# A swiglu's input product taken as seven products of quarters, in a two-block kernel of one core

## The chip, the core and the metric

The kernel runs on one core of one Trainium2 chip. Its time is the device time of one launch in microseconds (us), the median of several runs. TensorE is called PE, VectorE DVE, ScalarE ACT and GpSimd POOL, as in the profile; SP is the queue that starts the weight DMAs.

## The reference

Two transformer blocks follow each other. The first has two layers over 512 tokens and, in its first layer, 256 context tokens; each layer ends in a swiglu over a normed and modulated input. The second block (a short convolution, a dilated attention, a squared-relu MLP) isn't touched. What is changed here is the first product of this function, in both layers, with D = 1024 and FF = 2816:

```python
def swiglu(h, w_in, w_out):
    gt, up = jnp.split(h @ w_in, 2, axis=-1)
    return (jax.nn.silu(gt) * up) @ w_out
...
        hf = rms_norm(x, norm_ffn[l]) * (1.0 + sc_f) + sh_f
        x = x + g_f * swiglu(hf, ffn_w_in[l], ffn_w_out[l])
...
            hcf = rms_norm(ctx, norm_ffn[l]) * (1.0 + csc_f) + csh_f
            ctx = ctx + cg_f * swiglu(hcf, ffn_w_in[l], ffn_w_out[l])
```

## The kernel before, in words

Everything is float32. A product of two float32 matrices is made of three matmuls in a faster, rounded type (`fp32r`): each factor is split into a high part (a cast on ACT) and a low part (the rest, a subtraction on DVE), and high·high, high·low and low·high are added up in PSUM (`product`, L265, its matmuls on L273, L275 and L277).

**Weights.** `Weights` brings them in blocks of up to 2048 columns. `load` starts the DMA into one of two `wst` buffers, `split` casts it to `whi` on ACT (L91) and takes the low part `wlo` on DVE (L92), two buffers each, and `ahead` (L102) does both for the steps to come. The model is a list of steps (`Builder.step`, `Builder.run`); the instructions of the steps are then put in order on each engine by a scheduler, which looks at what depends on what, so that work of a later step can stand ahead of work of an earlier one.

**Tokens.** The activations lie transposed, as 8 tiles `x(k)` of 128 features by the tokens. Layer 0 has 768 of them (512 in `XT`, 256 in `XC`), layer 1 has 512.

**The input of the swiglu.** The last step of the mixer ahead of it calls `feed_mod(k, n)` for each tile k as soon as its residual is done. It adds the squares for the norm (ACT L327, then POOL L328) and makes the scaled tile's high part `nmh` (ACT L597) and low part `nml` (DVE L598). The scale by 1/rms comes after the product (`rstd`, `rbcast`, `nmr`), the shift as extra columns of the moving side.

**The swiglu (`swiglu`, L603).** Of the 2816 hidden features a tile has 128, so there are 22 tiles. For each one, a step `up` brings one weight block (8 k-tiles of the gate's columns and 8 of the up side's) and makes two products. In layer 0 that is 48 matmuls of 512 columns and 48 of 256 or 258; in layer 1 it is 96 of 256 or 258. DVE multiplies both results by `nmr` (L649), ACT takes the silu (L651), DVE adds the shift and multiplies (L652), and the result is split into `uh` and `ul`. The tiles come in parts of 8, 7 and 7; after each part four steps `down` multiply the part by the second weight matrix and add to the residual (L450). PE has enough to do in a `down` while the last tile's `uh` is finished, because the scheduler puts the next part's first `up` product ahead of it.

Of the kernel before, what the change touches and what calls it, by code (L numbers as in the profile page):

```python
# [45 lines left out]
def blk(w, k0, kt, c0, n):  # L46

    return w[k0 * P : (k0 + kt) * P, c0 : c0 + n].rearrange("(k p) n -> p k n", p=P), kt, n


def cols(views):

    ((h, l),) = views
    return [(h[:, :, c : c + P], l[:, :, c : c + P]) for c in range(0, h.shape[2], P)]


class Weights:
# [21 lines left out]
    def split(self, i):  # L79
        b = self.b  # L80
        nc = b.nc
        stage, n = self.loaded[i]
        self.loaded[i] = None
        desc, raw = self.desc[i]
        if raw:
            ((_, kt, m),) = desc
            self.done.append(stage[:, :n].rearrange("p (k n) -> p k n", k=kt))
            return
        hi = b.wpool.tile([P, 2048], FR, tag="whi", name="whi", bufs=WSP)
        lo = b.wpool.tile([P, 2048], FR, tag="wlo", name="wlo", bufs=WSP)  # L90
# [29 lines left out]
class Builder:  # L120
# [346 lines left out]
    def ada_first(self):  # L467
# [111 lines left out]
    def open_mod(self, l, side):  # L579


        n = L if l else T
        self.enter("nm", nm=(1, None, side))
        parts = [self.nm.tile([P, KT, n + 32], FR, name=m) for m in ("nmh", "nml")]
        self.feeds = parts + [self.nm.tile([P, n], F32, name="nmr"), self.nm.tile([P, KT, 4], F32, name="nmg")[:, :, 0:2]]
        self.gains(l, 1, self.feeds[3])
        self.split(self.M[:, l, 24:32, :], *(a[:, :, n : n + 2] for a in parts))

    def feed_mod(self, k, n):

        nc = self.nc
        hi, lo, _, G = self.feeds
        for z, (c0, m) in enumerate([(0, L)] + ([(L, C)] if n > L else [])):
            self.squares(k, c0, m, nc.gpsimd)
            g = G[:, k, z : z + 1]
            h = hi[:, k, c0 : c0 + m]
            nc.scalar.activation(h, self.x(k, c0, m), AF.Copy, scale=g)  # L597
            nc.vector.scalar_tensor_tensor(  # L598
                lo[:, k, c0 : c0 + m], self.x(k, c0, m), g, h.bitcast(F32), ALU.mult, ALU.subtract
            )  # L600


    def swiglu(self, l):  # L603
        wi, wo = self.I["ffn_w_in"][l], self.I["ffn_w_out"][l]
        n = T if l == 0 else L
        if l == 1:
            self.step(lambda: self.open_norm(("norm_mix_2", 0)))
        self.scope_step("ffn", hid=(1, None))

        if n == T:  # L610
            segs, at = [(0, L), (L, C + 2)], [(0, L), (L, T + 2)]
            tokens = lambda a: a[:, 0:T]
# [12 lines left out]
        parts = [(0, 8), (8, 7), (15, 7)]
        for q, (t0, nt) in enumerate(parts):

            def alloc():
                self.uh = self.hid.tile([P, 8, n], FR, tag="uh", name="uh")
                self.ul = self.hid.tile([P, 8, n], FR, tag="ul", name="ul")  # L630

            self.step(alloc)
            for i in range(nt):

                def up(v, i=i, start=q == 0 and i == 0):
                    nc = self.nc
                    rb = self.feeds[2]
                    og = product(v[0])
                    if start:
                        self.rstd(n)  # L640
                    ou = product(v[1])
                    if start:
                        nc.scalar.copy(rb, self.rbcast(n)[:, 0:n])
                    s, u = self.t(n), self.t(n)
                    sh = self.tmp.tile([P, 2, 2], F32, tag="sh", name="sh")
                    c = runs[0][1]
                    for y, o, d in ((0, og, s), (1, ou, u)):
                        nc.vector.tensor_copy(sh[:, y], o[:, c : c + 2])
                        nc.vector.tensor_tensor(tokens(d), tokens(o), tokens(rb), ALU.mult)  # L649
                    for z, (run, _) in enumerate(runs):  # L650
                        nc.scalar.activation(run(s), run(s), AF.Silu, bias=sh[:, 0, z : z + 1])  # L651
                        nc.vector.scalar_tensor_tensor(run(s), run(u), sh[:, 1, z : z + 1], run(s), ALU.add, ALU.mult)  # L652
                    self.split(s, self.uh[:, i, :], self.ul[:, i, :])

                self.step(up, (blk(wi, 0, KT, (t0 + i) * P, P), blk(wi, 0, KT, FF + (t0 + i) * P, P)))
            for i in range(0, KT, 2):

                def down(v, i=i, q=q, nt=nt):
                    if n == T:
                        outs = self.full(cols(v), self.uh, self.ul, 0, nt)  # L660
                    else:
                        o = self.pair(cols(v), self.uh, self.ul, 0, nt)
                        outs = [o[:, 0:L], o[:, L : 2 * L]]
                    for j in range(2):
                        k = i + j
                        self.residual(outs[j][:, 0:L], k, 0, L, self.mod(l, 5, k, 0))
                        if n == T:
                            self.residual(outs[j][:, L:T], k, L, C, self.mod(l, 5, k, 1))
                        if q == 2:
# [1670 lines left out]
```

## Time and profile before

| | |
|---|---|
| median of 3 runs | 3637.14 us (3633.1 to 3637.61) |
| profiled execution | 3626.45 us, its span 3624.4 us |
| PE busy | 3495.5 us (96%) |
| DVE busy | 1807.6 us (50%) |
| ACT busy | 1187.7 us (33%) |
| POOL busy | 72.0 us (2%) |
| chain of waits, by engine | PE 91%, DVE 4%, ACT 2%, DMA 1% |

The profile is one execution; its span runs from the first instruction to the last. An engine is busy while it executes an instruction. The rows called windows give the busy time of each engine in a stretch and the granted clock of PE there (1.00 is full speed). The chain of waits follows the end of the run back through what released each instruction.

### The profile page before, as it was taken

The page shows a single profiled execution, that of the slowest core. Times are in us where ns is not written, and L with a number is a line of the kernel's source. Part 1 is how long each engine was busy: PE and PEld are TensorE (multiplying, and loading weights), DVE is VectorE, ACT ScalarE, POOL GpSimd, SP SyncE. Part 2 cuts the span into 40 slices and gives each one's busy share as a digit, 9 for nine tenths or more (in the row PEclk, how much of TensorE's full clock was granted, in tenths as well). Part 3 has the DMA queues.
Part 4 walks back from the last instruction along what each step waited for, and adds up shares of the span by engine and source line. Part 5 has one row for each costly group of instructions (what it writes and reads, how often), then busy time and mean ns, then how long its engine had stood idle before and what let it go on. Part 6 is the DMA issues. An engine that isn't in the chain of part 4 may idle for free.

```text
span 3624.4 us, 46788 instructions
## 1 busy us (share of the span) xinstructions
PE 3495.5 (96%) x19754; PEld 3013.2 (83%) x19754; DVE 1807.6 (50%) x3145; ACT 1187.7 (33%) x1810; POOL 72.0 (2%) x87
## 2 busy tenths in 40 slices
PE   6999899999999989999999999999999999999998
PEld 4767777888888879988999888888889999988886
DVE  5657555653233345565444555444554444454445
ACT  4356545432121233343222322222334234222222
POOL 0000000020000001001000000000000000000000
PEclk9999999999999999999999999999999999999999
DMA  6111455422222223222333233333232222233332
GB/s 232 48 57 65 147 165 190 138 59 70 59 64 59 66 85 82 74 63 82 94 89 100 85 88 106 98 99 93 87 102 77 83 71 76 75 95 93 93 98 71
DMA packets 351873, 333.17 MB, mean 92 GB/s; under 512 B 22192, under 2 KB 293296, under 8 KB 351664
## 3 DMA queue, kind: packets, MB, share of 16 engines
q1 hardware_dynamic: 330320, 313.88, 27.8%
q10 hardware_dynamic: 21344, 16.30, 1.5%
q8 instruction: 155, 2.54, 0.3%
q14 instruction: 54, 0.44, 0.0%
HBM read 312.62 MB, written 15.96 MB: 91 GB/s over the span
## 4 chain that ended last, share of the span: by engine, by line
PE 91%; DVE 4%; ACT 2%; DMA 1%; issue 1%; SPq 0%; POOL 0%; ACTq 0%; DVEq 0%
PE ps L277 19%; PE ps L275 19%; PE ps L273 19%; PE ps L310 5%; PE ps L312 5%; PE ps L311 5%; PE ps L1332 3%; PE ps L1704 1%; PE ps L1705 1%; PE ps L1706 1%; PE psc L1332 1%; PE ds L986 1%; PE pp L273 1%; PE pp L275 1%; PE pa L515 1%
## 5 line engine op out<-in xcount | busy, mean ns | idle before, releaser
L91 ACT CAST whi<-wst 128x2048 fp32r<-128x2048 f32 (+5 forms) x245 | 442.1, 1805 | 1281.5 <-PE ps L275 910.9
L92 DVE TENSOR_TENSOR wlo<-wst,whi 128x2048 fp32r<-128x2048 f32 (+5 forms) x245 | 529.8, 2162 | 157.3 <-ACT whi L91 150.2
L275 PE MATMUL ps<-ul,whi 128*128 128x512 f32 (+1 forms) x1040 | 361.9, 375 | 0.0
L277 PE MATMUL ps<-uh,wlo 128*128 128x512 f32 (+1 forms) x1040 | 361.4, 375 | 0.0
L273 PE MATMUL ps<-uh,whi 128*128 128x512 f32 (+1 forms) x1040 | 359.8, 374 | 0.0
L277 PE MATMUL ps<-nhh,wlo 128*128 128x512 f32 x864 | 340.1, 394 | 0.0
L275 PE MATMUL ps<-nhl,whi 128*128 128x512 f32 x864 | 338.0, 392 | 0.0
L273 PE MATMUL ps<-nhh,whi 128*128 128x512 f32 x864 | 337.0, 390 | 0.0
L275 PE MATMUL ps<-nml,whi 128*128 128x258 f32 (+2 forms) x1408 | 322.7, 310 | 2.3 <-DVE nml L598 2.0
L273 PE MATMUL ps<-nmh,whi 128*128 128x258 f32 (+2 forms) x1408 | 319.9, 309 | 4.2 <-ACT nmh L597 4.2
L277 PE MATMUL ps<-nmh,wlo 128*128 128x258 f32 (+2 forms) x1408 | 322.5, 310 | 0.6 <-DVE wlo L92 0.6
L310 PE MATMUL ps<-whi,nhh 128*128 128x512 f32 x576 | 238.0, 413 | 0.0
L273 PEld LDWEIGHTS ps<-nmh,whi 128*128 128x128 f32 x1408 | 216.8, 188 | 20.8 <-issue 4.6
L275 PEld LDWEIGHTS ps<-nml,whi 128*128 128x128 f32 x1408 | 216.4, 189 | 18.4 <-DVE nml L598 4.1
L277 PEld LDWEIGHTS ps<-nmh,wlo 128*128 128x128 f32 x1408 | 216.7, 189 | 16.2 <-DVE wlo L92 0.9
L311 PE MATMUL ps<-wlo,nhh 128*128 128x512 f32 x576 | 230.2, 400 | 0.0
L312 PE MATMUL ps<-whi,nhl 128*128 128x512 f32 x576 | 229.9, 399 | 0.0
L275 PEld LDWEIGHTS ps<-ul,whi 128*128 128x128 f32 x1040 | 184.1, 188 | 38.3
L273 PEld LDWEIGHTS ps<-uh,whi 128*128 128x128 f32 x1040 | 183.0, 188 | 36.6
L277 PEld LDWEIGHTS ps<-uh,wlo 128*128 128x128 f32 x1040 | 183.6, 188 | 35.5
L275 PEld LDWEIGHTS ps<-nhl,whi 128*128 128x128 f32 x864 | 162.2, 188 | 37.5
L273 PEld LDWEIGHTS ps<-nhh,whi 128*128 128x128 f32 x864 | 162.2, 188 | 35.4
(439 smaller groups left out, 6037.1 us busy)
## 6 DMA issues: line engine op xcount, KB each, us to landing
wst<-in_ffn_w_in_dram SPq DMA_DIRECT2D x88, 512.0 KB, 4.9
wst<-in_ada_w_dram SPq DMA_DIRECT2D x42, 1024.0 KB, 5.2
wst<-in_attn_w_qkv_dram SPq DMA_DIRECT2D x36, 1024.0 KB, 5.1
wst<-in_mlp_w_up_dram SPq DMA_DIRECT2D x32, 1024.0 KB, 5.5
wst<-in_mlp_w_down_dram SPq DMA_DIRECT2D x32, 1024.0 KB, 5.0
wst<-in_even_w_in_dram SPq DMA_DIRECT2D x14, 1024.0 KB, 5.3
wst<-in_ffn_w_out_dram SPq DMA_DIRECT2D x16, 896.0 KB, 4.6
wst<-in_odd_w_in_dram SPq DMA_DIRECT2D x12, 1024.0 KB, 5.2
```

The lines of the kernel that those rows point to most:

```text
L91: nc.scalar.copy(hi[:, :n], stage[:, :n])
L92: nc.vector.tensor_tensor(lo[:, :n], stage[:, :n], hi.bitcast(F32)[:, :n], ALU.subtract)
L273: nc.tensor.matmul(outs[t][s], wh[:, k, :], xh[:, k0 + k, c0 : c0 + n], start=st, stop=False)
L275: nc.tensor.matmul(outs[t][s], wh[:, k, :], xl[:, k0 + k, c0 : c0 + n], start=False, stop=False)
L277: nc.tensor.matmul(outs[t][s], wl[:, k, :], xh[:, k0 + k, c0 : c0 + n], start=False, stop=sp)
L310: nc.tensor.matmul(o, lhs_h(4 * kk + k, 2 * i + j), wh[:, k, :], start=st, stop=False)
L311: nc.tensor.matmul(o, lhs_h(4 * kk + k, 2 * i + j), wl[:, k, :], start=False, stop=False)
L312: nc.tensor.matmul(o, lhs_l(4 * kk + k, 2 * i + j), wh[:, k, :], start=False, stop=sp)
L515: nc.tensor.matmul(ps[32 * k : 32 * k + 32, :], self.c2[:, a + 32 * k : a + 32 * k + 32], v[:, k, :], start=st, stop=sp,)
L986: nc.tensor.matmul(ps[:, o : o + w_], b.qkT[0][rows, h, j * P : (j + 1) * P], b.qkT[1][rows, h, c0 : c0 + w_], start=True, stop=True,)
L1332: mark = nc.tensor.matmul(out, lhsT, rhs, start=start, stop=stop)
L1704: nc.tensor.matmul(o, b.hh[:, k, at], wh[:, k, :], start=k == 0, stop=False)
```

## The change

Strassen's algorithm (in the form with seven products) replaces the plain product of a hidden tile. The weight block of a tile is seen as 2 by 2 quarters: a11 and a12 are the gate's columns of the first and the last four k-tiles, a21 and a22 the up side's. The input is seen as 2 by 2 quarters too: rows are the first or last four k-tiles, columns the first or the second half of the tokens (384 each in layer 0, 256 in layer 1), with two shift columns added. Seven products of quarters, each of 4 k-tiles and three matmuls, make 84 matmuls of 386 columns (layer 0) or 258 (layer 1).

- `combine` (new): for each tile POOL makes four sums of weight quarters, each 128x512, in `ws`, which has one buffer: s1 = a21+a22, s2 = s1−a11, s4 = a12−s2, s3 = a11−a21. Then seven factors of 512 columns are split (ACT L278, DVE L279) into both pairs of `whi` and `wlo`: a11, a12, s1 and s4 into the first, s2, s3 and a22 into the second.
- `quarters` (new, L323 ff.): the seven products in the order b11, t1, b21, b22, t2, t4, t3 of their input factor, into three PSUM regions R, Q and V, with copies from PSUM on ACT (L342, L344, L349, L353) and additions on DVE (L346, L350, L354, L355).
- `feed_mod`, through `scaled` and `factor`, now makes b11, t1, b21 and b22. A new step `mix_mod`, placed right ahead of the swiglu, makes t2, t4 and t3 in four rounds, from the scaled tiles of k and k+4, in four `t` tiles a round.
- The parts have 4 tiles in layer 0 (six parts, the last one of 2) and 6 in layer 1 (6, 6, 6 and 4). A `down` step has 4 tiles in layer 0 and 2 in layer 1. There are 96 residual additions in the swiglu of layer 0 (48 before) and 32 in that of layer 1 (24 before).

```diff
+        if raw == FAST:
+            self.done.append(self.combine(stage, desc))
+            return
...
+    def combine(self, stage, desc):
...
+        a11, a12, a21, a22 = (v[:, m, h] for m in range(2) for h in range(2))
+        ws = self.b.wpool.tile([P, 4, 4, P], F32, tag="ws", name="ws", bufs=1)[:, :, :q]
+        s1, s4, s2, s3 = (ws[:, i] for i in range(4))
+        nc.gpsimd.tensor_tensor(s1, a21, a22, ALU.add)
+        nc.gpsimd.tensor_tensor(s2, s1, a11, ALU.subtract)
+        nc.gpsimd.tensor_tensor(s4, a12, s2, ALU.subtract)
+        nc.gpsimd.tensor_tensor(s3, a11, a21, ALU.subtract)
+        out = {}
+        for names, srcs in ((("a11", "a12", "s1", "s4"), (v[:, 0], ws[:, 0:2])), (("s2", "s3", "a22"), (ws[:, 2:4], a22))):
...
+    def quarters(self, w, x, n, g, u):
...
+        one, two = self.ps(), self.ps()
+        R, Q, V = one[:, 0:n], one[:, L : L + n], two[:, 0:n]
...
+        add(R, "a11", "b11", True)
+        nc.scalar.copy(g[:, 0], R)
+        add(V, "s1", "t1", True)
+        nc.scalar.copy(u[:, 1], V)
+        add(Q, "a12", "b21", True)
+        nc.vector.tensor_tensor(g[:, 0], g[:, 0], Q, ALU.add)
+        add(V, "s4", "b22", False)
+        add(R, "s2", "t2", False)
+        nc.scalar.copy(g[:, 1], R)
+        nc.vector.tensor_tensor(g[:, 1], g[:, 1], V, ALU.add)
+        add(Q, "a22", "t4", True)
+        add(R, "s3", "t3", False)
+        nc.scalar.copy(u[:, 0], R)
+        nc.vector.tensor_tensor(u[:, 1], u[:, 1], R, ALU.add)
+        nc.vector.tensor_tensor(u[:, 0], u[:, 0], Q, ALU.add)
...
+        a, e = self.scaled(k, 0), self.scaled(k, 1)
+        if k < 4:
+            self.factor("b11", k, a)
+            nc.vector.tensor_tensor(e, e, a, ALU.subtract)
+            self.factor("t1", k, e)
+        else:
+            self.factor("b21", k, a)
+            self.factor("b22", k, e)
+
+    def mix_mod(self):
...
+        for k in range(4):
+            t = self.scaled(k, 0)
+            a, e = self.scaled(k + 4, 0), self.scaled(k + 4, 1)
+
+            b12 = self.scaled(k, 1)
+            nc.vector.tensor_tensor(t, b12, t, ALU.subtract)
+            nc.vector.tensor_tensor(t, e, t, ALU.subtract)
+            self.factor("t2", k, t)
+            nc.vector.tensor_tensor(t, a, t, ALU.subtract)
+            self.factor("t4", k, t)
+            nc.vector.tensor_tensor(t, e, b12, ALU.subtract)
+            self.factor("t3", k, t)
...
-        parts = [(0, 8), (8, 7), (15, 7)]
+        per = 4 if n == T else 6
+        parts = [(t0, min(per, FF // P - t0)) for t0 in range(0, FF // P, per)]
...
-            for i in range(0, KT, 2):
+            nb = 4 if n == T else 2
+            for i in range(0, KT, nb):
```

How it moves instructions, at three places. First, ACT at the start of layer 0's swiglu. L643 and the first L651 stand for the first hidden tile; before, nothing but a weight cast is between the last feed and them:

```order
L597 ACTIVATE nmh<-XC,nmg 128x256
L327 ACTIVATE t<-XT 128x512 [waits Pool_49]
L327 ACTIVATE t<-XC 128x256 [waits Pool_49]
L91 CAST whi<-wst 128x2048 [waits DMAHW5_49,DMAHW4_49,PE_49]
L643 COPY nmr<-ps 128x768 [waits PE_49]
L651 ACT_TABLE_LOAD
```

Now the same place; L342 and L344 are the copies out of PSUM of the first hidden tile, L676 and L677 make the scaled tiles of the last round of `mix_mod`, and L278 on `t2h`, `t4h`, `t3h` are its casts:

```order
L676 ACTIVATE t<-XT,nmg 128x128 [waits DVE_49]
L676 ACTIVATE t<-XC,nmg 128x256
L677 COPY t<-M 128x2
L278 CAST t2h<-t 128x386 [waits DVE_49]
L278 CAST t4h<-t 128x386 [waits DVE_49]
L342 COPY t<-ps 128x386 [waits Activation_49]
L278 CAST t3h<-t 128x386 [waits DVE_49]
L344 COPY t<-ps 128x386 [waits Activation_49]
L278 CAST whi<-wst 128x1024 [waits DMAHW2_49,PE_49]
L278 CAST whi<-ws 128x1024
L349 COPY t<-ps 128x386 [waits DVE_49,PE_49]
L751 ACT_TABLE_LOAD
```

The first tile's copy L342 now stands behind three of the four rounds of `mix_mod` and two thirds of the last one.

Second, DVE in one hidden tile of layer 1. Before:

```order
L648 COPY sh<-ps 128x2 [waits PE_49]
L649 TENSOR_TENSOR t<-ps,nmr 128x512
L648 COPY sh<-ps 128x2 [waits PE_49]
L649 TENSOR_TENSOR t<-ps,nmr 128x512
L652 SCALAR_TENSOR_TENSOR t<-t,sh 128x512 [waits DVE_49,Activation_49]
L92 TENSOR_TENSOR wlo<-wst,whi 128x2048 [waits DMAHW2_49,DMAHW1_49,Activation_49]
L243 TENSOR_TENSOR ul<-t,uh 128x512 [waits Activation_49]
```

Now, from the split of s2 and s3 of this tile to the split of a11 and a12 of the next one:

```order
L279 TENSOR_TENSOR wlo<-ws,whi 128x1024 [waits PE_49,Activation_49]
L279 TENSOR_TENSOR wlo<-wst,whi 128x512 [waits DMAHW4_49,Activation_49]
L354 TENSOR_TENSOR t<-t,ps 128x258 [waits Activation_49]
L355 TENSOR_TENSOR t<-t,ps 128x258
L747 TENSOR_TENSOR t<-t,nmr 128x2x256 [waits DVE_49]
L346 TENSOR_TENSOR t<-t,ps 128x258 [waits PE_49,Activation_49]
L752 SCALAR_TENSOR_TENSOR t<-t 128x256 [waits DVE_49]
L752 SCALAR_TENSOR_TENSOR t<-t 128x256
L279 TENSOR_TENSOR wlo<-wst,whi 128x1024 [waits DMAHW5_49,PE_49,Activation_49]
```

The weight split of the next tile, one instruction before, is now four, and its first one stands behind L747 and both L752, whose inputs all lie in SBUF.

Third, PE in a hidden tile of layer 0, at the end of the t2 product (`ps_7029` is this tile's PSUM with R and Q, `ps_7154` the next tile's; `whi_6750` holds s2, s3 and a22 of this tile, `whi_7015` a11 of the next):

```order
L336 MATMUL ps_7029<-t2l_6767,whi_6750 128x386
L336 MATMUL ps_7029<-t2h_6766,wlo_6751 128x386
L336 MATMUL ps_7154<-b11h_6412,whi_7015 128x386 [waits Activation_49]
L336 MATMUL ps_7154<-b11l_6413,whi_7015 128x386
L336 MATMUL ps_7154<-b11h_6412,wlo_7016 128x386 [waits DVE_49]
L336 MATMUL ps_7154<-b11h_6412,whi_7015 128x386
L336 MATMUL ps_7029<-t4h_6768,whi_6750 128x386 [waits Activation_49]
L336 MATMUL ps_7029<-t4l_6769,whi_6750 128x386
```

Four matmuls of the next tile's b11 product now stand ahead of this tile's last two products, t4 and t3, so these wait for the next tile's a11 and its low part.

## Rows read from the trace of the kernel before

**Rows 1.** The page: busy time, share of the span and instructions of three engines.

```profile
PE 3495.5 (96%) x19754; PEld 3013.2 (83%) x19754; DVE 1807.6 (50%) x3145; ACT 1187.7 (33%) x1810; POOL 72.0 (2%) x87
```

**Rows 2.** The page: the chain that ended last, share of the span by engine.

```profile
PE 91%; DVE 4%; ACT 2%; DMA 1%; issue 1%; SPq 0%; POOL 0%; ACTq 0%; DVEq 0%
```

**Rows 3.** Windows of seven hidden tiles each: first layer 0, then layer 1.

```profile
core 0: us, PE busy (x) PEld busy (x) DVE busy (x) ACT busy (x) POOL busy (x), PEclk, DMA share, GB/s
978.63:1096.24 117.61, 117.61 (x674) 103.03 (x673) 42.01 (x54) 25.96 (x28) 0.00 (x0) 1.00 0.20 60
1821.70:1901.04 79.34, 79.34 (x673) 79.34 (x672) 35.09 (x47) 21.57 (x20) 0.00 (x0) 1.00 0.30 89
```

**Rows 4.** Windows over the start of the swiglu, layer 0, then layer 1.

```profile
766.00:793.00 27.00, 24.14 (x139) 19.98 (x138) 19.09 (x31) 11.81 (x19) 11.45 (x8) 1.00 0.28 79
1676.00:1692.00 16.00, 11.83 (x76) 10.89 (x75) 14.35 (x17) 6.99 (x10) 10.06 (x6) 0.89 0.25 71
```

**Rows 5.** Groups by line and shape, ACT: count, busy us, mean ns.

```profile
L91 ACT CAST whi<-wst 128x1024 fp32r<-128x1024 f32 x9 | 9.5, 1053 | 44.1 <-PE ps L275 38.4 <-issue 5.6
L327 ACT ACTIVATE t<-XT 128x512 f32<-128x512 f32 x76 | 47.1, 624 | 59.2 <-DVE XT L450 25.5 <-DVE XT L768 25.1 <-DMA XT<-in_xT_dram 4.7
L327 ACT ACTIVATE t<-XC 128x256 f32<-128x256 f32 x21 | 8.0, 405 | 2.6 <-DVE XC L450 2.0 <-POOL acc L328 0.5
L597 ACT ACTIVATE nmh<-XT,nmg 128x512 fp32r<-128x512 f32 x16 | 11.4, 710 | 6.4 <-DVE XT L450 6.4
L1506 ACT COPY vv<-ps 128x384 f32<-128x384 f32 x32 | 15.2, 478 | 18.1 <-PE ps L1332 17.8
L1402 ACT ACTIVATE kg<-ktm,st 128x128 f32<-128x128 f32 x48 | 15.0, 395 | 1.3 <-PE psc L1332 1.2
```

**Rows 6.** Groups by line and shape, DVE.

```profile
L243 DVE TENSOR_TENSOR ul<-t,uh 128x1024 fp32r<-128x1024 f32 x32 | 38.8, 1219 | 0.0
L243 DVE TENSOR_TENSOR ul<-t,uh 128x512 fp32r<-128x512 f32 x22 | 15.1, 684 | 0.1
L652 DVE SCALAR_TENSOR_TENSOR t<-t,sh 128x512 f32<-128x512 f32 x44 | 33.1, 752 | 4.5
L652 DVE SCALAR_TENSOR_TENSOR t<-t,sh 128x256 f32<-128x256 f32 x22 | 10.5, 478 | 0.0
L92 DVE TENSOR_TENSOR wlo<-wst,whi 128x2048 fp32r<-128x2048 f32 x195 | 447.2, 2293 | 130.9 <-ACT whi L91 128.2
```

**Rows 7.** Groups by line and shape, POOL.

```profile
L328 POOL TENSOR_TENSOR acc<-acc,t 128x512 f32<-128x512 f32 x14 | 24.5, 1751 | 548.2 <-PE ps L277 365.2 <-ACT t L327 182.7
L1689 POOL TENSOR_TENSOR B<-al,fconsts 128x512 f32<-128x512 f32 x12 | 15.8, 1346 | 120.5 <-DVE z L1782 58.1 <-DVE z L1779 36.6 <-DMA al<-in_rpbr_dram 16.9
```

**Rows 8.** Timeline of DVE and of POOL at layer 1's start: start, us, instruction.

```profile
1682.15 3.21 DVE L92 TENSOR_TENSOR wlo<-wst,whi 128x2048 fp32r<-128x2048 f32 x1
1685.28 4.12 DVE L598 SCALAR_TENSOR_TENSOR nml<-XT,nmg,nmh 128x512 fp32r<-128x512 f32 x3
...
1681.93 6.26 POOL L328 TENSOR_TENSOR acc<-acc,t 128x512 f32<-128x512 f32 x3 [1.58 <-ACT t L327]
```

**Rows 9.** Timeline of PE behind three of its gaps [idle before <-releaser].

```profile
1682.54 0.48 PE L273 MATMUL ps<-nmh,whi 128*128 128x256 f32 x2 [4.17 <-ACT nmh L597]
...
512.12 1.22 PE L1332 MATMUL psc<-z,Pm 128*128 128x128 f32 x4 [3.13 <-ACT qs L1568]
...
549.74 2.02 PE L1332 MATMUL ps<-us,rowsel 128*128 128x192 f32 x8 [3.21 <-ACT us L242]
```

**Rows 10.** Windows over those gaps and what follows them; PEclk is the granted clock.

```profile
1680.00:1685.00 5.00, 2.46 (x13) 2.50 (x14) 5.00 (x4) 4.67 (x7) 3.35 (x3) 0.79 0.02 5
1685.00:1690.00 5.00, 5.00 (x37) 4.79 (x37) 4.40 (x4) 0.00 (x0) 3.11 (x2) 0.87 0.69 196
...
509.00:516.00 7.00, 3.88 (x20) 2.91 (x20) 5.19 (x17) 2.18 (x7) 0.00 (x0) 0.76 0.36 135
546.00:553.00 7.00, 3.79 (x21) 2.33 (x20) 1.90 (x5) 4.48 (x11) 0.00 (x0) 0.76 0.49 190
```

More of the change, by code (lines that the diff above doesn't have):

```diff
@@ L24 @@
 WST = 2
+FAST = "fast"
 WSP = 2
@@ L88, in split @@
             return
-        hi = b.wpool.tile([P, 2048], FR, tag="whi", name="whi", bufs=WSP)
-        lo = b.wpool.tile([P, 2048], FR, tag="wlo", name="wlo", bufs=WSP)
+        hi, lo = self.parts()
         nc.scalar.copy(hi[:, :n], stage[:, :n])
@@ L107, in ahead @@
         while len(self.done) < min(len(self.desc), self.pos + WSP):
-            if self.taken and not self.desc[len(self.done)][1]:
+            if self.taken and self.desc[len(self.done)][1] is not True:
                 break
@@ L285, in pair, with add @@
         return ps
+    def quarters(self, w, x, n, g, u):
+        nc = self.nc
+        one, two = self.ps(), self.ps()
+        R, Q, V = one[:, 0:n], one[:, L : L + n], two[:, 0:n]
+        def add(o, a, b, first):
+            (wh, wl), (xh, xl) = w[a], x[b]
+            kt = wh.shape[1]
+            for k in range(kt):
+                for i, (c, d) in enumerate(((wh, xh), (wh, xl), (wl, xh))):
+                    nc.tensor.matmul(
+                        o, c[:, k], d[:, k, :n], start=first and k + i == 0, stop=k == kt - 1 and i == 2,
+                        skip_group_check=not first,
+                    )
+        add(R, "a11", "b11", True)
[13 more added lines that the diff above has]
+        nc.vector.tensor_tensor(u[:, 0], u[:, 0], Q, ALU.add)
     def full(self, tiles, xh, xl, k0=0, kt=KT, first=True, last=True):
@@ L583, in open_mod @@
         self.enter("nm", nm=(1, None, side))
[L584 to L587, printed above, removed]
+        self.side = side
+        self.half = n // 2
+        self.fx = {}
+        self.factors(self.nm, ("b11", "t1", "b21", "b22"))
@@ new lines, in open_mod, with factors, scaled @@
+        self.rb = self.nm.tile([P, n], F32, name="nmr")
+        self.G = self.nm.tile([P, KT, 4], F32, name="nmg")[:, :, 0:2]
+        self.gains(l, 1, self.G)
+        self.shift = self.M[:, l, 24:32, :]
+    def factors(self, pool, names):
+        for x in names:
+            self.fx[x] = [pool.tile([P, 4, self.half + 8], FR, name=x + p)[:, :, : self.half + 2] for p in "hl"]
+    def scaled(self, k, z):
+        nc = self.nc
+        m = self.half
+        t = self.t(m + 2)
+        for c0, c1, c in ((0, L, 0), (L, T, 1)):
+            a, e = max(c0, m * z), min(c1, m * (z + 1))
+            if a < e:
+                nc.scalar.activation(t[:, a - m * z : e - m * z], self.x(k, a, e - a), AF.Copy, scale=self.G[:, k, c : c + 1])
+        nc.scalar.copy(t[:, m : m + 2], self.shift[:, k, :])
+        return t
@@ L636, in up @@
                     nc = self.nc
-                    rb = self.feeds[2]
-                    og = product(v[0])
+                    s, u = (self.t(2 * m + 4).rearrange("p (z n) -> p z n", z=2) for _ in range(2))
+                    self.quarters(v, self.fx, m + 2, s, u)
                     if start:
                         self.rstd(n)
[L641 to L652, printed above, removed]
@@ L653, in up @@
-                    self.split(s, self.uh[:, i, :], self.ul[:, i, :])
-                self.step(up, (blk(wi, 0, KT, (t0 + i) * P, P), blk(wi, 0, KT, FF + (t0 + i) * P, P)))
-            for i in range(0, KT, 2):
-                def down(v, i=i, q=q, nt=nt):
[L659 to L664, printed above, removed]
+                        nc.scalar.copy(self.rb, self.rbcast(n)[:, 0:n])
@@ L665, in down @@
+                    h, l = (x[:, i, :].rearrange("p (z n) -> p z n", z=2) for x in (self.uh, self.ul))
+                    self.split(s[:, :, 0:m], h, l)
+                self.step(up, (blk(wi, 0, KT, (t0 + i) * P, P), blk(wi, 0, KT, FF + (t0 + i) * P, P)), raw=FAST)
+            nb = 4 if n == T else 2
+            for i in range(0, KT, nb):
+                def down(v, i=i, q=q, nt=nt):
+                    tiles = cols(v)
+                    for j in range(nb):
                         k = i + j
-                        self.residual(outs[j][:, 0:L], k, 0, L, self.mod(l, 5, k, 0))
@@ L670, in down @@
+                        if n == T:
+                            self.residual(outs[j % 2][:, L:T], k, L, C, self.mod(l, 5, k, 1))
+                        if q == len(parts) - 1:
                             if n == T:
```

74 lines of the change are left out of this document (47 added, 27 removed).

## The prediction

> **What bounds the kernel now.** I read the page's busy shares first. PE is busy 96% of the span, DVE half of it, ACT a third, POOL 2% [rows 1]. The chain that ended last runs through PE for 91% [rows 2]. So the time is PE's work plus the places where it idles, and a change that takes matmuls away can gain, as long as the engines that feed PE keep up. The windows over the swiglu show how it stands there: for seven hidden tiles in a row PE is busy all the time at full clock, DVE 36% to 44% of it and POOL not at all [rows 3]. At the start of each swiglu PE idles for 2.9 us in layer 0 and 4.2 us in layer 1 [rows 4, 9].
>
> **What it takes off PE.** A tile took 117.61/7 = 16.80 us in layer 0 and 79.34/7 = 11.33 us in layer 1 [rows 3]. Layer 1's 96 matmuls of some 257 columns give 0.118 us each; layer 0's other 48, of 512, then take (16.80 − 48·0.118)/48 = 0.232. On the line between them 386 columns cost 0.176 and 258 cost 0.1186. The order shows 84 matmuls a tile in place of 96, so I don't doubt that the work leaves: 84·0.176 = 14.75 and 84·0.1186 = 9.96. That saves 2.05·22 = 45 us and 1.37·22 = 30 us: **−75**.
>
> **What it adds at the start of each swiglu.** ACT's rows give a line: 0.405 us at 256 columns and 0.624 at 512, so 0.52 for 386, 0.41 for 258 and 0.19 for almost none; a scaled tile is 0.09 dearer, 0.61 for 384 and 0.49 for 256, and 128 columns are 0.395 [rows 5].
>
> - The last four feeds, one after the other on ACT: in layer 0 one took 0.62 + 0.41 + 0.71 + 0.49 = 2.2 us. Now it is squares 1.03, scaled tiles 0.61 + 0.40 + 0.49 with 0.19 twice, two casts 1.04: 3.95. Four of them: +7. In layer 1 it is 1.33 against 0.62 + 2·0.68 + 0.82 = 2.8: +6.
> - `mix_mod`, a round: ACT makes four scaled tiles (0.80, 0.80, 1.08, 1.08) and three casts (1.56), 5.3 us; DVE does seven operations of 386, on the line of L243 0.55 each, 3.9 us [rows 6]. Each cast waits for a subtraction and each low part for a cast, and a round holds its four tiles until the end. All overlapped it is 5.3, all in a row 9.2; I take the middle, 7.3, so 29 us for four rounds. In layer 1: ACT 4·0.68 + 3·0.41 = 3.95, DVE 7·0.42 = 2.9, middle 5.4, so 22 us.
> - All of this lies on the path. The first tile's copy L342 stands behind the last round's casts on ACT, and the b21 product waits for that copy. PE has only the b11 and t1 products meanwhile, 24 matmuls: 4.2 us and 2.8.
>
> Layer 0: 7 + 29 − 4 = +32; layer 1: 6 + 22 − 3 = +25. **+57** together.
>
> **What the clock adds.** PE came back from gaps of 4.17, 3.13 and 3.21 us [rows 9] with a granted clock of 0.79 and 0.87 in the next two windows, and 0.76 in windows over the other two [rows 10]. That is matmuls at 1.2 GHz in place of 2.4 for part of the stretch: (0.21 + 0.13)·5 = 1.7 us, or 0.24·7 = 1.7. I charge 1.7 us for each gap of about 3 us or more: twice at the starts, **+3**. The Trainium skill's page "TensorE: Matmul & The Clock Gate", section "HAM oscillation — how this bites in real kernels", describes a loop that idles between its bursts and is throttled anew on every round; the trace has no such loop, only single gaps. With that rule my sum is what stands below, without it some 44 us less.
>
> **Layer 1's steps.** The four sums are new work for POOL. Alone, a 128x512 addition took 1.35 us; the feeds' ones, beside DVE, 1.75 [rows 7]. In the one place where both engines work from SBUF at once, three took 6.26 us, 2.1 each, and DVE's low part of 2048 columns 3.21 instead of 2.29, three L598 4.12 where L652, of that shape, takes 0.75 (2.25 in all) [rows 6, 8]. So the two hold each other up. Four sums take 5.4 us alone and 8.3 at that rate; I take 6.1, nearer to the lower end, as DVE has fewer such operations in a tile than there.
>
> Now the loop from one t3 product's end to the next: ACT casts s2 and s3 (1.05, [rows 5]), DVE takes their low parts (1.22, [rows 6]), which frees the only `ws`; POOL makes the next tile's sums (6.1); DVE's L747 and L752, held up by these, end some 0.3 later; then comes the next tile's first low part (1.22), for which PE waits ahead of t4, two matmuls and a copy (0.75), and t4 and t3 (24·0.1186 = 2.84). Sum 13.5 us, where PE has 9.96 of work: 3.5 us idle, then 1.7 for the clock. Of 22 tiles 18 follow another one in their part: 18·5.2 = **+94**.
>
> **Layer 0's steps.** The same loop gives 1.05 + 1.22 + 6.1 + 0.3 + 1.22 + 0.9 + 4.2 = 15.0 against 14.75: balanced. But t2 waits for L346, which stands on DVE behind the previous tile's three L752. From t3's end: copy 0.48 [rows 5], two additions 1.1, L747 0.95, silu 0.6, three L752 1.45, L346 0.55: 5.1 us, and up to 10.5 if each of the four SBUF operations waits for one sum of POOL. PE has 44 matmuls before t2, 7.7 us. So between nothing and 2.8 us; I take 2.0, since POOL starts its sums right before. There are 16 such pairs; in about ten POOL has a next tile to form: **+21**.
>
> Six ends of a part: before, the next part's first tile covered the last `uh`; now both weight buffers belong to one tile, and the cover is three k-tiles of the first `down`, 18 matmuls of 512 and 18 of 256, 6.3 us. The path is 4.6 without L346, cast 0.85, low part 0.95, and a weight split of 2.29 on DVE in between [rows 6]: 8.7, with one wait for POOL up to 10. I take 3 us and 1.7 of clock each: +28, and the last part, with two tiles, has two k-tiles less cover: +4. **+32**. The 56 more residual additions cost nothing: they run on DVE while PE works on `down`, 8 us a pair of tiles against some 2.5 of additions (by L652's durations, [rows 6]); without that cover they would be 35 us.
>
> **Sum.** −75 + 57 + 3 + 94 + 21 + 32 = +132 us: 42 in layer 0, 90 in layer 1. Against the profiled execution's 3626 us this is 3758; the runs' median is 11 us above it, so I predict **3769 us**.
>
> **Rivals.**
>
> - *The clock doesn't fall in the loop* (0.13). Every granted clock under 1 that I found stands behind a single gap [rows 10]; a loop may differ. Then 18·1.7 + 6·1.7 + 3 = 44 us go: 3725.
> - *DVE isn't held up by POOL* (0.13). For it: the only evidence is one stretch of 7 us [rows 8]. Then the low part of a11 is not behind the sums, the loop fits into PE's work, and t2's waits vanish; the starts and half of the ends of parts stay: −75 + 60 + 25 = +10: 3647. The Trainium skill's page "SBUF — State Buffer", section "Who interferes with whom", says that a DVE instruction with two SBUF inputs and a GpSimd instruction that reads SBUF exclude each other for a whole instruction; the trace's stretch agrees in kind, both being done in 7.5 us where their work in a row would be 8.6.
> - *Faster* (0.09): PE's saving is kept. One place decides, the wait for the next tile's a11 ahead of t4: if the sums with their waits delay it by no more than 2.5 us in place of 6.1, the loop closes in 9.96. POOL can't be that fast [rows 7], so it takes DVE going ahead of POOL and the ends of parts covered by three k-tiles: −75 + 60 = −15: 3622. Against it speaks what rows 8 show of DVE.
> - *The sums at the rate of rows 8* (0.08): 8.3 in place of 6.1 makes layer 1's loop 2.2 longer, +40, and layer 0's 17.2, 2.4 over PE's work in 16 pairs, +38, instead of its 21: 3826.
>
> **How the numbers follow.** The main case has 0.57. Its own range takes the ends of `mix_mod` (5.3 to 9.2 and 3.95 to 6.9 a round: ±14 in all), of the sums (5.4 to 7), and of t2's wait (0 to 2.8): 3722 to 3807. Together with the first two rivals it holds 0.83, so the range is 3645 to 3815. Slower by over 0.2% (7 us, about what can be told from no change) are the main case, the first and the last rival and most of the second: 0.85. Faster: the third and a little of the second, 0.11. Same: 0.04.
>
> **What would show it.** PE's matmul work in seven tiles near 103 and 70 us; an idle stretch of PE of 30 us or so at the start of each swiglu, with the b21 product released by ACT's L342; in layer 1 a gap of 3 to 4 us in each tile ahead of t4's or b11's matmuls, released by DVE's low part L279, and a granted clock of 0.8 to 0.9 in those windows; layer 0's tiles at 15 to 17 us. I would be wrong if layer 1's tiles took 10 to 11 us, if POOL's sums lay near 1.35 us with DVE's operations at their old durations, or if PE had work through `mix_mod`.

## The result and the profile after

The changed kernel takes 3757.28 us (median of 4 runs, 3754.41 to 3761.31), the kernel before 3637.38: a ratio of 1.0332, with a 95% interval of 1.0314 to 1.0349. It is 120 us slower; 132 were forecast.

The page's busy shares and its chain of waits, which answer to [rows 1, 2]:

```profile
PE 3467.1 (92%) x19226; PEld 3018.9 (80%) x19226; DVE 2113.3 (56%) x3539; ACT 1384.6 (37%) x2340; POOL 338.7 (9%) x263
...
PE 79%; DVE 10%; ACT 5%; issue 2%; DMA 2%; POOL 1%; SPq 0%; ACTq 0%; DVEq 0%; POOLq 0%
```

PE lost 28 us of busy time, and the chain of waits now runs through DVE and ACT for 15%, where it was 6% [rows 2]. Windows over the two swiglus, the same stages in both kernels, show where the time is. Before, layer 0's swiglu with the feeds ahead of it and layer 1's (span, then PE, PEld, DVE, ACT, POOL, clock, DMA share, GB/s):

```profile
757.90:1332.72 574.82, 571.96 (x3258) 498.45 (x3256) 214.36 (x279) 125.66 (x140) 18.79 (x14) 1.00 0.21 61
1678.37:2058.95 380.58, 376.41 (x2657) 352.83 (x2658) 171.66 (x218) 104.80 (x101) 7.76 (x5) 1.00 0.31 91
```

After, the same two stages, and then each of them cut in two at the first b21 product:

```profile
757.91:1388.76 630.85, 552.47 (x3000) 514.42 (x3000) 388.48 (x490) 232.18 (x406) 148.35 (x98) 0.94 0.19 56
1737.66:2199.91 462.25, 376.76 (x2394) 345.76 (x2394) 301.74 (x397) 194.63 (x355) 134.92 (x89) 0.92 0.26 75
757.91:828.29 70.38, 27.91 (x121) 23.83 (x121) 39.85 (x70) 44.04 (x120) 20.43 (x18) 0.65 0.06 15
828.29:1388.76 560.47, 524.56 (x2880) 490.60 (x2880) 348.63 (x421) 188.15 (x286) 127.92 (x80) 0.98 0.20 61
1737.66:1782.80 45.14, 9.28 (x41) 8.72 (x40) 26.13 (x57) 26.82 (x86) 12.78 (x9) 0.58 0.09 24
1782.80:2199.91 417.11, 367.48 (x2353) 337.04 (x2354) 275.61 (x341) 167.81 (x269) 122.14 (x80) 0.95 0.28 80
```

Layer 0 became 56.0 us longer, layer 1 81.7. PE's busy time fell by 19.5 us in layer 0 and not at all in layer 1, where 10% fewer matmuls (2394 for 2657) kept it busy as long. PE's idle time rose from 2.9 to 78.4 us and from 4.2 to 85.5. (The untouched rest of the program is 7 us shorter, so the two spans differ by 131 us; between the medians it is 120. In the second block alone the last 7000 matmuls take 10 us less: 1534 to 1536 us in the traces of all 13 changed kernels, 1546 in the one trace of the kernel before. No run shows why.)

Who PE waited for, in layer 0 from the feeds on, then in layer 1 (us in total, times, longest):

```profile
PE ps L336 <- ACT t L342: 25.6, 1, 25.6
PE ps L336 <- DVE t L346: 18.1, 10, 1.8
PE ps L309 <- ACT uh L278: 17.0, 6, 3.0
...
PE ps L488 <- POOL acc L398: 4.2, 1, 4.2
...
PE ps L336 <- DVE wlo L279: 39.2, 14, 2.9
PE ps L336 <- ACT t L342: 19.4, 1, 19.4
PE ps L336 <- ACT whi L278: 8.4, 3, 2.8
PE ps L488 <- POOL acc L398: 8.4, 1, 8.4
PE ps L336 <- ACT b11h L278: 5.3, 1, 5.3
```

These are the waits of the forecast in their places: the start's b21 behind L342, ten waits of t2 for L346, six ends of parts, and 17 waits in layer 1's loop. Of these 17, 14 are for the low part of the next tile's a11; the three for `whi`, one in the first pair of tiles of the second to fourth part, are for the cast of the next tile's sums, ahead of its t1 product. One round of `mix_mod` on the chain of waits of layer 0's start (start us, us, what), up to the next round's first scaled tile:

```profile
807.38 0.52 ACT t L676
...
810.85 0.52 ACT t2h L278
...
811.39 0.57 DVE t2l L279
...
811.99 0.57 DVE t L711
...
812.58 0.52 ACT t4h L278
...
813.13 0.57 DVE t4l L279
...
813.73 0.57 DVE t L713
...
814.32 0.51 ACT t3h L278
814.84 0.52 ACT t L676
```

814.84 − 807.38 = 7.46 us: ACT and DVE take turns, and nothing of the next round begins before the last cast. Then one hidden tile of layer 1 on DVE, on POOL and on PE:

```profile
1941.59 1.53 DVE L747 TENSOR_TENSOR t<-t,nmr 128x512 f32<-128x512 f32 x1
1943.15 2.81 DVE L752 SCALAR_TENSOR_TENSOR t<-t 128x256 f32<-128x256 f32 x2
1945.88 1.21 DVE L279 TENSOR_TENSOR wlo<-wst,whi 128x1024 fp32r<-128x1024 f32 x1
...
1939.69 1.62 POOL L121 TENSOR_TENSOR ws<-wst 128x512 f32<-128x512 f32 x1 [7.76 <-DVE wlo L279]
1941.28 1.28 POOL L124 TENSOR_TENSOR ws<-wst 128x512 f32<-128x512 f32 x1
1942.53 1.74 POOL L122 TENSOR_TENSOR ws<-ws,wst 128x512 f32<-128x512 f32 x1
1944.35 1.33 POOL L123 TENSOR_TENSOR ws<-wst,ws 128x512 f32<-128x512 f32 x1
...
1947.14 0.39 PE L336 MATMUL ps<-b11h,wlo 128*128 128x258 f32 x1 [2.88 <-DVE wlo L279]
```

POOL's sums run from 1939.69 to 1945.68, 6.0 us. DVE's L747 takes 1.53 us where its shape takes 0.68, the two L752 2.81 where they would take 0.96 [rows 6]; each ends 0.3 to 0.6 us behind the end of a sum. The low part that PE waits for starts right after.

### The profile page after: what moved, and what is told of

It reads as the page before. It is cut to its first block, busy times and chain, and to the rows that moved or that the text cites. A ratio compares the mean times of both kernels' runs of the same rounds, so it can differ in the third digit from the quotient of the medians.

```text
span 3755.2 us, 47005 instructions
## 1 busy us (share of the span) xinstructions
PE 3467.1 (92%) x19226; PEld 3018.9 (80%) x19226; DVE 2113.3 (56%) x3539; ACT 1384.6 (37%) x2340; POOL 338.7 (9%) x263
## 4 chain that ended last, share of the span: by engine, by line
PE 79%; DVE 10%; ACT 5%; issue 2%; DMA 2%; POOL 1%; SPq 0%; ACTq 0%; DVEq 0%; POOLq 0%
PE ps L309 12%; PE ps L313 12%; PE ps L311 12%; PE ps L336 10%; PE ps L380 4%; PE ps L382 4%; PE ps L381 4%; PE ps L1437 3%; DVE t L752 2%; PE ps L1809 1%; PE ps L1810 1%; PE ps L1811 1%; ACT whi L278 1%; PE psc L1437 1%; DVE wlo L279 1%
## 5 line engine op out<-in xcount | busy, mean ns | idle before, releaser
L95 ACT CAST whi<-wst 128x2048 fp32r<-128x2048 f32 (+5 forms) x205 | 359.1, 1752 | 866.4 <-PE ps L311 642.1
L96 DVE TENSOR_TENSOR wlo<-wst,whi 128x2048 fp32r<-128x2048 f32 (+5 forms) x205 | 430.5, 2100 | 179.2 <-ACT whi L95 177.1
L313 PEld LDWEIGHTS ps<-nhh,wlo 128*128 128x128 f32 x864 | 162.2, 188 | 36.3
L518 DVE TENSOR_TENSOR XT<-ps,XT 128x512 f32<-128x512 f32 x80 | 51.6, 686 | 236.3 <-PE ps L313 236.3
L121 POOL TENSOR_TENSOR ws<-wst 128x512 f32<-128x512 f32 x44 | 74.3, 1688 | 1207.9 <-DMA wst<-in_ffn_w_in_dram 733.5
L520 DVE SCALAR_TENSOR_TENSOR XT<-ps,M,XT 128x512 f32<-128x512 f32 x110 | 80.4, 747 | 172.4 <-PE ps L313 171.9
L279 DVE TENSOR_TENSOR wlo<-ws,whi 128x1024 fp32r<-128x1024 f32 x88 | 108.0, 1227 | 112.7 <-ACT whi L278 112.5
L381 PEld LDWEIGHTS ps<-wlo,nhh 128*128 128x128 f32 x576 | 156.2, 271 | 7.1
```

Source lines behind the costliest of these rows:

```text
L279: self.nc.vector.tensor_tensor(lo, src, hi.bitcast(F32), ALU.subtract)
L313: nc.tensor.matmul(outs[t][s], wl[:, k, :], xh[:, k0 + k, c0 : c0 + n], start=False, stop=sp)
L381: nc.tensor.matmul(o, lhs_h(4 * kk + k, 2 * i + j), wl[:, k, :], start=False, stop=False)
L520: self.nc.vector.scalar_tensor_tensor(x, ps, scale, x, ALU.mult, ALU.add)
```

## The experiments

Each run is set against the kernel before on the same chip; "e1" and so on are their names. Where a kernel leaves work out, its expectation says which. The kernel before had medians of 3628 to 3633 us there and 3637 beside the change, so a difference between the medians of two such groups of runs can be off by up to 9 us. The ratios are taken within one group; where the two differ by more than a few us, both are given.

**e1: no sums.**

```diff
-        nc.gpsimd.tensor_tensor(s1, a21, a22, ALU.add)
...
-        for names, srcs in (... (v[:, 0], ws[:, 0:2])), (... (ws[:, 2:4], a22))):
+        for names, srcs in (... (v[:, 0], v[:, 1])), (... (v[:, 0], a22))):
```

> Leaves out POOL's four sums of weight quarters: a21 and a22 of the loaded block are split in the place of s1 and s4, a11 and a12 once more in the place of s2 and s3, so the output is not the reference's; every cast, low part and matmul stays. This prices the sums. Theory (the sums, and DVE's operations that they hold up, set layer 1's loop and layer 0's wait of t2): layer 1's tiles at PE's own 10 to 10.9 us without the gaps of 2.9, layer 0's gaps of 1.8 gone: -39 - 8 - 18 us of idle and some 20 of clock, so about 3670 us (3655 to 3690). Rival (the seven splits themselves are too much for DVE and ACT, the sums only add waiting that is hidden): gaps of 2 us or more stay in layer 1, above 3715 us.

3649.91 us, ratio 1.0047 (1.0031 to 1.0063): 107 us less than the change (104 by the ratios), 5 below the range. A tile of layer 0, then one of layer 1, in windows:

```profile
952.00:967.06 15.06, 15.06 (x86) 14.82 (x85) 9.89 (x14) 7.43 (x12) 0.00 (x0) 1.00 0.20 70
...
1856.78:1868.14 11.36, 10.63 (x84) 10.21 (x84) 8.39 (x14) 6.18 (x12) 0.00 (x0) 1.00 0.35 96
```

All waits of t2 are gone, and of the 17.0 us at the ends of parts 1.9 are left, which I hadn't expected: those too came from POOL. And layer 1's tile, with no sums at all, takes 11.36 us, against 11.33 before [rows 3]. PE is busy for 10.63 of them and waits for 0.64 for a11's low part, so seven products of 258 columns save nothing there, at least with R and Q in one buffer; buffers of their own (e12, below) were not tried without the sums.

**e3: memsets in place of the sums.**

```diff
-        nc.gpsimd.tensor_tensor(s1, a21, a22, ALU.add)
...
+        for o in (s1, s2, s4, s3):
+            for _ in range(3):
+                nc.gpsimd.memset(o, 0.01)
```

> Each of POOL's four sums is replaced by three memsets of the same 128x512 piece of ws, so the factors s1 to s4 are constants and the output is not the reference's. POOL is still in the chain (it waits for the low parts of s2 and s3, and the casts wait for it) and still works some 1.4 to 2 us a piece, but reads nothing from SBUF. Theory (DVE is held up by POOL where both read SBUF): L747 and L752 return to 0.7 and 0.5 us, POOL's work alone fits, layer 1's tiles take 10 to 11 us: 3660 to 3690. Rival (the chain through the one ws buffer sets the loop, whatever POOL does to DVE): layer 1's tiles stay at 13.5 us or more and the time within 15 us of 3757.

3658.64 us, ratio 1.0068 (1.0051 to 1.0086), a little below the range. By its groups in layer 1 POOL was as busy as with the sums, 12 · 0.526 = 6.3 us a tile against 6.0, and stood in the same chain, but L746 and L751 (the change's L747 and L752) were back at their old durations. Its groups, then the same two operations in the change:

```profile
L746 DVE TENSOR_TENSOR t<-t,nmr 128x512 f32<-128x512 f32 x32 | 22.1, 692 | 0.9
L751 DVE SCALAR_TENSOR_TENSOR t<-t 128x256 f32<-128x256 f32 x32 | 14.0, 480 | 0.6
...
L123 POOL MEMSET ws<- 128x512 f32 x240 | 113.5, 526 | 240.8 <-DVE wlo L278 240.8
...
L752 DVE SCALAR_TENSOR_TENSOR t<-t 128x256 f32<-128x256 f32 x40 | 40.1, 1043 | 0.6
L747 DVE TENSOR_TENSOR t<-t,nmr 128x512 f32<-128x512 f32 x38 | 33.9, 892 | 0.9
```

So it is not POOL's time in the chain that costs nearly 100 us but its reading beside DVE. POOL's time in the chain is worth the 9 us between e1 and e3.

**e2: sums made, not used.** The factors as in e1, the four sums as in the change.

> POOL still makes its four sums into ws, but nothing reads them: a21 and a22 of the loaded block are split in the place of s1 and s4, a11 and a12 in the place of s2 and s3 (the output is not the reference's). So POOL leaves the chain and goes on reading SBUF beside DVE. Theory (holding DVE up is enough by itself): L747 and L752 of layer 1 still take twice their time or more, DVE has some 11 us of a tile, layer 1's tiles stay over 11.9 us and the time is 3670 to 3730. Rival (the hold-up costs only because POOL's sums are also waited for): as without sums, 3642 to 3660.

3701.93 us, ratio 1.0197 (1.0178 to 1.0217): the hold-up alone costs 52 us over e1 (55 by the ratios); the other 55 (49) come only when the sums are waited for as well. A tile of layer 1 took 12.67 us, DVE busy 10.68 of it (8.39 in e1); below it the low part of 512 columns and L752 in layer 1:

```profile
1905.32:1917.99 12.67, 11.04 (x85) 10.32 (x85) 10.68 (x14) 6.08 (x12) 6.40 (x5) 1.00 0.30 83
...
L279 DVE TENSOR_TENSOR wlo<-wst,whi 128x512 fp32r<-128x512 f32 x21 | 28.5, 1359 | 0.0
L752 DVE SCALAR_TENSOR_TENSOR t<-t 128x256 f32<-128x256 f32 x44 | 19.4, 482 | 0.6
```

Which of DVE's operations are hit depends on when POOL starts. Here the sums waited only for the weight block's DMA, and the weights' low parts and L747 took the loss, not L752, which I had expected to be hit as well.

**e4: no `mix_mod`**, t2, t4 and t3 taken from b11, b21 and b22; **e7: neither sums nor `mix_mod`**.

```diff
+        for a, b in (("t2", "b11"), ("t4", "b21"), ("t3", "b22")):
+            self.fx[a] = self.fx[b]
```

> Leaves out mix_mod: the products t2, t4 and t3 use the factors b11, b21 and b22, so the output is not the reference's. Theory (mix_mod lies bare on the path at the start of both swiglus): PE's waits of 25.6 and 19.4 us ahead of the first b21 product go but for 1 or 2 us each, and some of the half clock behind them: -42 to -50, about 3711 us (3703 to 3718). Rival (the feeds and the norm's sum hold PE there anyway): no more than 20 us, 3737 or more.

> Leaves out both POOL's sums (as in the kernel without sums) and mix_mod (as in the kernel without it); the output is not the reference's. What is left is the seven products with their splits, copies and additions. Theory (the two account for the whole loss and touch different places): 3757 - 107 - 57 = 3593 us (3584 to 3602), below the kernel before by some 40, that is the 75 of PE's work less the feeds, the norm's sum and the longer ends. Rival (they share something, say the clock or the start): 3605 or more.

e4: 3699.86 us, ratio 1.0181 (1.016 to 1.0202), 57 less than the change (55 by the ratios) and a little below its range; e7: 3598.48, ratio 0.9912 (0.9891 to 0.9934). The two add up: 107 + 57 = 164 alone, 159 together (104 + 55 and 153 by the ratios). What is left is a gain of 30 us over the kernel before (3628.43), all that the seven products would bring with the weights' sums and `mix_mod` for nothing. Two things that every one of these kernels has are priced by no run: the smaller parts, and a `dynamic_dma_scratch_size` of 1024, which the change sets where the kernel before leaves the default.

**e8: two rounds of `mix_mod` in flight**, two scaled tiles in one `t` buffer.

```diff
+            o = [x[:, c : c + m] for x in (self.t(), self.t()) for c in (0, L)]
```

> Two scaled tiles share one t buffer in mix_mod, so that the four buffers hold two rounds; same arithmetic. Theory (a round took 7.36 us in layer 0 because the next round's scaled tiles wait for its buffers; ACT alone has some 5.3 us of work in it, DVE 3.9): the waits ahead of the first b21 fall from 25.6 and 19.4 us to about 18 and 13: -10 to -16 us, 3741 to 3748. Rival (casts and subtractions wait for one another anyway): less than 4 us.

3734.97 us, ratio 1.0285 (1.0264 to 1.0307), 22 less than the change (17 by the ratios). PE's waits at the two starts, 25.6 and 19.4 us in the change, in e8's timeline of PE:

```profile
814.09 0.69 PE L336 MATMUL ps<-b21h,whi 128*128 128x386 f32 x1 [12.77 <-ACT t L342]
...
1769.03 0.58 PE L336 MATMUL ps<-b21h,whi 128*128 128x258 f32 x1 [9.86 <-ACT t L342]
```

They fell by 22.4 us together, where I had worked out 14: with two rounds open, ACT makes the next round's scaled tiles while DVE is still at this one's, and the two no longer take turns.

**e6: the next tile's b11 behind t3** on PE.

```diff
+            if self.t3_last is not None:
+                order.enter_context(self.tc.issue_after(self.t3_last.ins))
             add(R, "a11", "b11", True)
```

> Same arithmetic; on PE the first product of a hidden tile (b11) is kept behind the last matmul of the tile ahead of it, so the four matmuls that stood ahead of t4 go behind t3. Theory (PE stalls because these four wait for the next tile's a11 while t4 and t3 are ready): the low part of a11 is done some 10 us after t3's end, PE's work between is 10 to 10.8, so layer 1's gaps fall from 2.9 to under 0.7 us: -37 to -45 and 15 to 20 of clock, about 3700 us (3685 to 3715). Layer 0's gaps of 1.8 ahead of t2 stay. Rival (the loop is set by the sums in any order): the same gap stands ahead of the next tile's b11, 3745 to 3760.

3764.28 us, ratio 1.0361 (1.0345 to 1.0378): nothing gained, rather 7 to 11 us lost; the rival had it, at a little over its range. PE's waits in layer 1, and ACT's timeline ahead of one of them:

```profile
PE ps L337 <- ACT t L354: 52.6, 18, 3.3
```

```profile
1948.13 0.62 ACT L279 CAST uh<-t 128x512 fp32r<-128x512 f32 x1 [4.14 <-DVE t L757]
1948.66 1.04 ACT L279 CAST whi<-wst 128x1024 fp32r<-128x1024 f32 x1
1949.60 1.04 ACT L279 CAST whi<-ws 128x1024 fp32r<-128x1024 f32 x1
1950.55 0.36 ACT L354 COPY t<-ps 128x258 f32<-128x258 f32 x1
```

t4 writes Q, the other half of the buffer in which R lies, and so waits for R's second copy (L354, the change's L349). On ACT that copy stands behind a cast of `uh`, which waits for DVE's L757, which waits for POOL, and behind the cast of the sums. The late sums reach PE by a second way, which my step had hidden behind the first: in the change too, t4 starts at 1947.88, right behind the copy L349 (1947.46 to 1947.83).

**e5, e10, e11: the sums on DVE**, alone, with e6's order, and with e8's buffers too.

```diff
-        nc.gpsimd.tensor_tensor(s1, a21, a22, ALU.add)
+        nc.vector.tensor_tensor(s1, a21, a22, ALU.add)
```

> The four sums are made on DVE in place of POOL, all else as in the change, same result. Theory (not the adding but the two engines' hold-up costs): a sum takes 0.68 us on DVE, DVE has 9.0 + 2.7 = 11.7 us in a tile of layer 1 and 13.6 in layer 0, so layer 1's tiles take 11.7 to 12.6, layer 0's stay near PE's work: 3655 to 3695. Rival (DVE was the bound of the loop all along): its tiles in layer 1 take 13.5 us or more, 3735 or more.

> The sums on DVE as in the kernel with sums on DVE, and on PE the next tile's b11 and t1 kept behind this tile's t3, same result. Theory (that kernel was slow because PE's order put the next tile's b11 and t1 matmuls ahead of this tile's own ready products, not because DVE lacks the time): in layer 1 the loop is cast 1.05, low parts 1.9, additions 0.8, three sums, L747 and both L752 3.7, cast 1.05, copy 0.37, t4 and t3 2.84, together 11.8 us against the 13.75 of the change; layer 0 near PE's work: 3660 to 3690. Rival (DVE's own load is what it cost): 3740 or more, as with the sums on DVE alone.

> The former kernel with two rounds of mix_mod in flight as well, same result: the best version that keeps the seven products here. Theory (the start and the loop are separate): 20 to 24 us less than the former one, so about 3652 us (3638 to 3670), still not below the kernel before. Rival (one of them covers the other): less than 10 us apart.

3781.99 us (ratio 1.0423, 1.0399 to 1.0448), 3797.88 (1.0469, 1.0452 to 1.0486) and 3773.35 (1.0403, 1.0384 to 1.0422): all slower than the change. For e5 and e10 neither theory had it right; e11 came 24.5 us below e10, close to the 20 to 24 of its theory, but both lie over 100 us above their ranges. DVE was not full in e5, 35.8 us of 60 in layer 1; the queues' order changed. The longest waits of PE in layer 1, e5 first:

```profile
PE ps L336 <- ACT whi L278: 44.6, 32, 2.5
```

```profile
PE ps L337 <- DVE t L351: 68.1, 14, 4.9
```

In e5's timeline PE has the next tile's b11 and part of its t1 ahead of this tile's t2, t4 and t3. In e10 that order is put right, and now L351 (the addition of Q, for which t2 waits) stands on DVE behind the next tile's sums and low parts: 4.9 us a tile (DVE is busy for 10.6 of a tile's 17.2 us).

**e12: R, V and Q in buffers of their own; e13: that and e8.** Sums on POOL.

```diff
-        one, two = self.ps(), self.ps()
-        R, Q, V = one[:, 0:n], one[:, L : L + n], two[:, 0:n]
+        R, V, Q = (self.ps()[:, 0:n] for _ in range(3))
```

> R, V and Q each get a PSUM buffer of their own (before, R and Q were halves of one), same arithmetic. So b21 need not wait for the copy of R, t2 not for the addition of Q, t4 not for the second copy of R; the order now also has b11 behind t3. The sums stay on POOL. Theory (PE meets the late sums through waits that the shared buffer adds; what must wait is t3, for the copy behind the sums' cast): in layer 1 the loop is 1.05 + 1.22 + 6.1 + 1.05 + 0.37 + 1.42 = 11.2 us, so tiles of 11.2 to 11.7 in place of 13.75, layer 0 loses its gaps of 1.8, each start gains 24 matmuls: -37 -18 -7 and some 10 of clock, about 3685 us (3670 to 3705). Rival (the hold-up on DVE sets the loop whichever product waits): tiles in layer 1 of 13 us or more, above 3730.

> The former kernel with two rounds of mix_mod in flight as well, same result. Theory: 15 to 22 us less than the former one (the start's waits were 25.6 and 19.4 us and fell by 12.8 and 9.5 when tried alone), about 3666 us (3648 to 3690), still above the kernel before, since what is left of the starts and of the ends of parts is more than the 40 us or so that layer 0's products save. Rival: it comes below the kernel before, under 3625.

3687.05 us (ratio 1.0156, 1.0139 to 1.0173) and 3664.87 (1.0095, 1.008 to 1.011). A tile of layer 1 in e12 and PE's largest wait in its loop:

```profile
1890.52:1902.54 12.02, 10.89 (x85) 10.26 (x85) 10.93 (x14) 6.07 (x11) 6.10 (x4) 1.00 0.32 87
```

```profile
PE ps L335 <- ACT t L348: 15.9, 17, 1.9
```

The wait that is left is the one that must be, t3's for the copy behind the sums' cast, now 0.9 us on average. POOL and DVE hold each other up as before (DVE busy 10.93); it just reaches PE less. Of the change's 120 us 57 are left; what is gone (70 us between the medians, 64 by the ratios) went with the halves of one PSUM buffer that waited for one another, and with b11 behind t3, as e12's timeline has it, which alone (e6) gained nothing. e13 is the fastest of the kernels that make all the factors, and still slower than the kernel before. None beats it.

## Why the prediction was right, and where its terms were off

The direction and the places of the waits were right, and layer 1 lost more than layer 0, as forecast (42 and 90 us forecast, 56.0 and 81.7 measured). By terms; PE's work is measured by e1's tiles, the idle terms by the windows of the profiled execution, and the last row is what is left of PE's busy time:

| term | forecast | measured |
|---|---|---|
| PE's work | −75 | −54 |
| idle at the starts | +57 | +71 |
| layer 1's loop, idle | +63 | +50 |
| layer 0's t2 and ends of parts, idle | +43 | +36 |
| half clock, and what else is left | +44 | +35 |
| sum | +132 | +138 |

That the sum came within 6 us is partly luck: PE's work and the starts cost 35 us more than forecast, the other three terms 29 us less. (The ten waits of 2.0 us in layer 0's term are 20 us, not the 21 that stand there.)

- **PE's work** was the largest miss. "84·0.176 = 14.75 and 84·0.1186 = 9.96" takes a product's matmuls to run on without a break. By e1's windows a tile has 15.06 us of PE in layer 0 and 10.63 in layer 1: −1.74·22 = −38 and −0.70·22 = −15. In layer 0, where PE doesn't wait in that tile, a product takes some 2.14 us, 0.178 a matmul in place of 0.176. In layer 1 a product without a break takes 1.44 us, 0.120 a matmul; the rest are three places in a tile (b11's low part, t4 and b21) where PE starts anew. There the second matmul starts 0.22 us after the first, where the others follow at 0.12, and b21 starts 0.38 us after t1's last one, waiting for the copy.
- **The starts**: windows give 42.5 − 2.9 = 39.6 us and 35.9 − 4.2 = 31.7, where I had 32 and 25. The rounds were right (7.3 forecast, 7.46 measured). What was missing are the norm's own steps on PE. PE waits 4.2 and 8.4 us for the squares that its sum L488 adds up. POOL's queue is a part of that, since the first tile's sums stand ahead of the last squares on it: without the sums, in e1, PE waits 1.4 and 4.0 us there, so they cost 2.8 and 4.4. Behind it PE waits 3.1 and 2.8 us for DVE's part of the norm (L413). I hadn't gone through either.
- **Layer 1's loop** is 13.75 us, with 13.5 forecast, and the sums' 6.1 measured 6.0. Its idle part is smaller (2.9 in place of 3.5), since PE's work in the tile is longer. That the wait is one of a11 alone was wrong, as e6 shows: the copy on ACT would have held PE as long.
- **Layer 0**: ten waits of 1.8 us for L346 (2.0 forecast) and five of the six ends of parts at 3.0 (3.0). The ends had a wait for POOL as a mere addition; e1 and e3 show that without the hold-up only one wait of 1.9 us is left of them, and e2, with the hold-up alone, has all 17.0.
- **The clock** fell less often in layer 1's loop. Of the 35 us, worked out as PE's busy time over what e1's tiles would need, 16 are in layer 1, where I had 32, and 19 in layer 0, where I had 12; layer 0's start ran at 0.65. Of the 17 waits in layer 1's loop, of 2.3 to 2.9 us, 10 were followed by work at full clock and 7 by a stretch at 0.71 to 0.88. With the same gap of 2.88 us ahead:

```profile
1816.97:1833.23 16.26, 13.27 (x84) 12.85 (x85) 11.07 (x14) 6.28 (x12) 5.90 (x4) 0.81 0.24 66
...
1933.40:1947.14 13.74, 10.78 (x84) 10.28 (x84) 11.06 (x14) 6.29 (x12) 5.90 (x4) 1.00 0.28 78
```

So the rival "the clock doesn't fall in the loop" was half right. The Trainium skill's page "TensorE: Matmul & The Clock Gate", section "HAM oscillation — how this bites in real kernels", has its loop throttled on every round, behind waits that it gives as some 3 to 5 us. The traces agree for e10, where each of the 14 waits in layer 1's loop, of 4.84 to 4.91 us, was followed by a stretch at 0.75 to 0.88; in the change 10 of the 17 waits were not.

The rival without a hold-up at 3647 is borne out as a price, not as a case: e3, where POOL reads nothing, is at 3659. The Trainium skill's page "SBUF — State Buffer", section "Who interferes with whom", names DVE instructions with two SBUF inputs beside GpSimd instructions that read SBUF, and not ones that only write it; e3 agrees (0.48 us for L752 beside memsets, 1.04 on average beside sums). That the two exclude each other for a whole instruction is more than the prediction's stretch shows: 7.5 us is less than the 8.6 of the work in a row, so some of it overlapped.

## What to carry to other kernels

Fewer matmuls are a gain only for what remains between restarts and waits: price each product's start, and follow the new operands through every engine's queue from end to end, the small engines' queues too. Here sums on POOL that read SBUF held up DVE's operations with two SBUF inputs, even when nobody waited for the sums: in e2 DVE was busy 10.68 us a tile, where e1 without the sums has 8.39. Where independent results are halves of one PSUM buffer, a wait for one is in this kernel a wait for both; separate buffers, with the order that came with them, took 64 to 70 us off here.

## What was not expected of the hardware

A memset of 128x512 on POOL (0.53 us) left DVE's operations at their durations; a sum of the same shape took L752 from 0.48 to 1.04 us and L747 from 0.69 to 0.89, on average. In e2 the loss moved to other instructions on DVE (a low part of 512 columns took 1.36 us instead of 0.68), though POOL's work was the same. Behind equal gaps PE lost clock in some rounds of layer 1's loop and not in others; what decides that stays open.
